# Three inner output projections of a four-layer trunk: the last block's second tile in two column halves, its pre-norm in one VectorE step

## The chip, the cores and the metric

One Trainium2 chip, one core. The metric is the device time of one execution of the program in microseconds (us). A profile of one execution accompanies the times; all rows below are of that execution. Engines are called PE (TensorE), DVE (VectorE), ACT (ScalarE), POOL (GpSimd) and SP (the queue that issues most loads).

## What is computed

A trunk of four layers on x (512 positions, 1024 channels, float32), each layer with another token mixer:

```python
for i in range(4):
    h = rmsnorm(x, pre_norm[i])
    y = branch_i(h, ...)          # mixer and gate, then  (...) @ w_out
    x = x + rmsnorm(y, post_norm[i])
```

```python
def rmsnorm(x, g):
    xf = x.astype(jnp.float32)
    y = xf * lax.rsqrt(jnp.mean(xf * xf, axis=-1, keepdims=True) + EPS)
    return (y * g.astype(jnp.float32)).astype(x.dtype)
```

The change is in the seam between two layers: the product with `w_out` (1024 x 1024), the post-norm and residual, and the pre-norm of the next layer. There are three such inner seams (behind layers 0, 1 and 2) and an outer one at the end, which has no next layer.

## The kernel before

**Arithmetic.** Every float32 matrix product is made of three TensorE products of rounded parts: a tensor `a` is split into `aH` (a rounded copy, by ACT) and `aL = a - aH` (by DVE or POOL), and `aH bH + aH bL + aL bH` is accumulated in a PSUM bank. Activations are kept transposed as `XH` and `XL`, by blocks of 128 positions.

**Weights.** They come as a stream of chunks in one fixed order. SP loads a chunk into one of two `wraw` buffers; a split puts it into a pair `wh`, `wl` (two pairs, and one more pair of buffers for chunks with the tag "x"). For some chunks the split is cut in four parts and the subtraction is spread: "mix" gives the four parts to POOL, DVE, POOL, DVE; "late" gives all four to POOL, and its casts go to ACT two at a time. In the seam, the chunks c0 and c1 hold the first 512 output columns, c2 and c3 the second 512 (each chunk holds half of the contraction); c2 has the tag "x". The next layer's first chunk ("mix") and second chunk ("late", tag "x") are split while block 3 is computed, by `split_later` (L168), which hands out the steps one by one.

**The projection, `out_proj` (L317).** Loop `t` runs over four blocks of 128 positions, and once more (t = 4) to finish the last. A block has two output tiles of 128 x 512 (n = 0 and 1), each of 24 matmuls: 12 with one chunk, 12 with the other. The engines run pipelined over blocks: in pass t, PE computes block t's tiles and transposes block t-2; u = t-1 is the block whose norm is being finished, v = t-2 the block that is transposed.

Names along the path of block 3, in their order:

- `y_stat(t, n)` (L357): ACT squares a PSUM tile and sums it into `ssq`; `y_gain` (L360): DVE multiplies the tile by the post-norm gain into `yg`.
- `y_root(t)` (L365): nine small DVE instructions of 128 x 1, each waiting for the one before, give the root `rs[t]`.
- `x_new(t, n)` (L368): DVE updates the residual, `xt = yg * rs + xt`.
- `x_stat(t, n)` (L373): ACT squares the new half of x; POOL multiplies it by the next layer's gain into `hblk`.
- `x_root(t)` (L380): nine small DVE instructions again; `x_scale(t, n)` (L383): ACT scales `hblk` by the root.
- `transposes` (L268): eight PE transposes of a block, in two banks; `x_high` (L277): ACT copies them into `XH`; `x_low` (L281): DVE writes `XL`.

In pass 4 PE has no tile of the projection left. It runs the first tiles of the next layer's first product on blocks 0 and 1 (`nxt`), one in each of three places, then the transposes of block 3, then a fourth such tile.

**Order.** Instructions through `act_`, `dve_`, `pool_`, `pe_` keep the order in which they are written, each on its engine; the rest is placed by a planner. All of `out_proj` except casts and subtractions of some chunks is written out this way. PSUM has eight banks; `bank()` takes a free one. `last_tile` (L331), for the outer projection alone, already computes its second tile of block 3 in two column halves.

Of the kernel before, what the change touches and what calls it, by code (L numbers as in the profile page):

```python
# [10 lines left out]
F32 = mybir.dt.float32  # L11
# [3 lines left out]
AF = mybir.ActivationFunctionType  # L15
ALU = mybir.AluOpType
MUL, ADD, SUB, MAX = ALU.mult, ALU.add, ALU.subtract, ALU.max
# [30 lines left out]
def tile_hybrid_trunk(ctx: ExitStack, tc: tile.TileContext, I, out, depth=4):  # L48
# [22 lines left out]
    act_, dve_, pool_, pe_ = (Engine(e, True) for e in engines)  # L71
# [14 lines left out]
    sm = ctx.enter_context(tc.tile_pool(name="sm", bufs=8))  # L86

    def bank():
        return ps.tile([128, 512], F32, name="bank", tag="bank")
# [78 lines left out]
    def split_later():  # L168

        i = state["split"]  # L170
        if i == len(stream):
            return iter(())
        if state["load"] == i:
            do_load(stream[i])
            state["load"] += 1
        state["split"] += 1
        stream[i]["steps"] = split_steps(stream[i])
        return stream[i]["steps"]
# [102 lines left out]
    def x_low(bvs, t, dve=dve):  # L281
        for kk, bv in enumerate(bvs):
            dve.tensor_tensor(out=XL[:, t, 4 * kk:4 * kk + 4, :], in0=bv,
                              in1=XH[:, t, 4 * kk:4 * kk + 4, :].bitcast(F32), op=SUB)
# [32 lines left out]
    def out_proj(pre, x, begin, tail, emit_x, nxt):  # L317


        ssq = [sm.tile([128, 2], F32, name="ssq") for t in range(4)]  # L320
        yg, hs, sss, rs, bvs = {}, {}, {}, {}, {}
        more = nxt is not None
        roots = bank()

        def cs(n):
            return slice(512 * n, 512 * n + 512)

        def mms(*a, **kw):
            out_mms(*pre.S, *a, **kw)
# [24 lines left out]
        def junk():  # L354
            return yp.tile([128, 512], BF16, name="junk", tag="junk", bufs=2)[:]
# [4 lines left out]
        def y_gain(t, n, bt):  # L360
            y = yg0[:, t, :] if n == 0 else yp.tile([128, 512], F32, name="yg1", bufs=2)[:]
            dve_.tensor_tensor(out=y, in0=bt[:], in1=gpost[:, cs(n)], op=MUL)
            yg[t, n] = y
# [9 lines left out]
        def x_stat(t, n):  # L373
            if n == 0:
                hs[t] = yp.tile([128, 1024], F32, name="hblk", tag="hblk", bufs=2)
                sss[t] = sm.tile([128, 2], F32, name="ssq")
            act_.activation(out=junk(), in_=x[:, t, cs(n)], func=AF.Square, scale=1.0 / 32, accum_out=sss[t][:, n:n + 1])
            pool_.tensor_tensor(out=hs[t][:, cs(n)], in0=x[:, t, cs(n)], in1=gpre[:, cs(n)], op=MUL)

        def x_root(t):  # L380
            rs[t] = rsqrt(sss[t][:, 0:1], 1, 1.0, 1, sss[t][:, 1:2], dve_, pb=roots[:, 8 * t + 4:8 * t + 7])

        def x_scale(t, n):  # L383
            act_.activation(out=hs[t][:, cs(n)], in_=hs[t][:, cs(n)], func=AF.Copy, scale=rs[t])

        while len(pre.bts) < 4:
# [5 lines left out]
        yp, gpost, gpre = begin()  # L392
        yg0 = yp.tile([128, 4, 512], F32, name="yg0")
        c1, c2 = get(), get()
        w = split_later()
        for t in range(5 if more else 4):

            u, v = t - 1, t - 2
            if t == 0:
                for _ in w:  # L400
                    pass
                c3 = get()
            if u >= 0:
                y_stat(u, 1, bt)
                y_root(u)
            if more and v >= 0:
                x_scale(v, 1)
            if t == 4:
                for _ in w:
                    pass  # L410
            if t < 4:
                mms(bts[t], t, 1, c1, True, range(2))
            else:
                next(nxt, None)
            if more and v >= 0:
                bvs[v] = transposes(hs[v], pe_)
            if t < 4:
                mms(bts[t], t, 1, c1, True, range(2, 4))
            else:
                next(nxt, None)  # L420
            if more and v >= 0:
                x_high(bvs[v], v, act_)
            if t < 4:
                y_stat(t, 0, bts[t])
            if u >= 0:
                x_new(u, 0)
                y_gain(u, 1, bt)
                if more:
                    x_stat(u, 0)
                x_new(u, 1)  # L430
                if more:
                    x_stat(u, 1)
            if t < 4:
                y_gain(t, 0, bts[t])
            if t == 3 and not more:
                last_tile()
                break
            if t < 4:
                bt = bank()
                mms(bt, t, 0, c2, False)  # L440
                if t == 3 and more:
                    w = split_later()
            if more and u >= 0:
                x_root(u)
            if more and v >= 0:
                x_low(bvs[v], v, dve_)
            for _ in w:
                pass
            if t < 4:
                mms(bt, t, 1, c3, True)  # L450
            else:
                next(nxt, None)
            if more and u >= 0:
                if t == 3:
                    w = split_later()
                    next(w, None)
                    next(w, None)
                x_scale(u, 0)
        if more:
            x_scale(3, 1)  # L460
# [1613 lines left out]
```

## Time and profile before

| | us |
|---|---|
| median of three runs | 989.39 |
| the two lower of these runs | 989.27, 989.39 |
| the profiled execution | 988.71 |
| its span, first to last instruction | 986.9 |
| PE busy (matmuls) | 949.0 |
| DVE, ACT, POOL busy | 619.3, 510.6, 444.7 |

The mean granted clock of TensorE is 0.985 of full speed. A row of a timeline gives the start of an instruction from the beginning of the span, its duration, engine, line, operation, what it writes and reads, its shape, how many follow each other as one row (x2), and in brackets the engine's idle time before it with what ended it. Where a helper records the operation, the line is that of the helper (L66); the tile names tell the instructions apart: `bank<-ssq` is the first instruction of a root, `xt<-yg,rs_y,xt` is x_new, `XL<-bank,XH` is x_low, `wl<-wraw,wh` a weight split, `hblk<-hblk,rs_y` is x_scale. A second instruction can be recorded as starting a little before the end of the one ahead of it.

### The profile page before, as it was taken

Reading aid. Unit: us, or ns where it says so; the run is one execution under the profiler, and the core shown is the slowest. Engines: PE = TensorE matmul, PEld = TensorE weight load, DVE = VectorE, ACT = ScalarE, POOL = GpSimd, SP = SyncE. Lnnn points to the kernel's source line nnn. Section 1 sums busy time; section 2 is a strip of 40 time slices with the busy share of each in tenths; the row PEclk is TensorE's granted clock in tenths of the full one; section 3 lists DMA queues with packets and bytes.
Section 4 is the critical chain, followed back from the end, with each engine's and each line's share of the span. In section 5 each row is a group of like instructions: output and inputs, shape, how many; then the busy total and the mean of one; then the engine's idle time right before and its main releaser. Section 6 shows DMA issues by size and latency. Waiting matters only on the chain.

```text
span 986.9 us, 14348 instructions
## 1 busy us (share of the span) xinstructions
PE 949.0 (96%) x5319; PEld 784.0 (79%) x5319; DVE 619.3 (63%) x1431; ACT 510.6 (52%) x1133; POOL 444.7 (45%) x337
## 2 busy tenths in 40 slices
PE   7959999999999999999999999999999999999997
PEld 6858988778889888887897877778767778888876
DVE  7899796855686866676820345666576857314365
ACT  4547777734367665663643243675683752222231
POOL 6677585656554131333646351714364535411120
PEclk8979999999999999999999999999999999999998
DMA  9211111435418232123124422110126033323021
GB/s 243 83 43 44 44 43 44 171 124 122 149 62 217 86 128 86 43 86 129 45 80 136 121 66 72 48 50 20 67 70 232 27 103 100 114 93 120 6 81 65
DMA packets 69366, 90.40 MB, mean 92 GB/s; under 512 B 13608, under 2 KB 49584, under 8 KB 69168
## 3 DMA queue, kind: packets, MB, share of 16 engines
q1 hardware_dynamic: 66944, 80.63, 26.6%
q10 hardware_dynamic: 2352, 8.85, 2.4%
q8 instruction: 42, 0.69, 0.3%
q14 instruction: 28, 0.23, 0.1%
HBM read 83.44 MB, written 4.98 MB: 90 GB/s over the span
## 4 chain that ended last, share of the span: by engine, by line
PE 74%; DVE 14%; ACT 5%; issue 3%; POOL 3%; DMA 0%; POOLq 0%; ACTq 0%; DVEq 0%; SPq 0%
PE bank L66 22%; PE bank L218 9%; PE bank L217 9%; PE bank L216 9%; PE bank L1841 4%; PE bank L1842 4%; PE bank L1843 4%; PE bank L101 4%; PE bank L1731 3%; DVE bank L66 2%; DVE xt L66 2%; PE bank L1773 2%; PE bank L1524 1%; DVE wl L66 1%; DVE rs_y L66 1%
## 5 line engine op out<-in xcount | busy, mean ns | idle before, releaser
L160 POOL TENSOR_TENSOR wl<-wraw,wh 128x2048 fp32r<-128x2048 f32 (+3 forms) x37 | 139.2, 3767 | 250.7 <-ACT wh L156 231.8
L216 PE MATMUL bank<-XH,wh 128*128 128x512 f32 (+1 forms) x526 | 183.2, 350 | 0.1
L218 PE MATMUL bank<-XH,wl 128*128 128x512 f32 (+1 forms) x526 | 181.5, 345 | 1.1 <-POOL wl L160 0.9
L217 PE MATMUL bank<-XL,wh 128*128 128x512 f32 (+1 forms) x526 | 181.0, 344 | 0.7 <-DVE XL L1660 0.7
L66 POOL TENSOR_TENSOR wl<-wraw,wh 128x512 fp32r<-128x512 f32 (+1 forms) x63 | 93.8, 1513 | 93.3 <-ACT wh L66 74.7
L66 PE MATMUL bank<-wh,XH 128*128 128x512 f32 (+1 forms) x328 | 114.0, 360 | 0.8 <-ACT g L66 0.8
L66 PE MATMUL bank<-wl,XH 128*128 128x512 f32 (+1 forms) x328 | 111.3, 352 | 0.3
L218 PEld LDWEIGHTS bank<-XH,wl 128*128 128x128 f32 x526 | 99.1, 188 | 15.2 <-POOL wl L160 1.5
L66 PE MATMUL bank<-wh,XL 128*128 128x512 f32 (+1 forms) x328 | 110.4, 349 | 0.6 <-POOL XL L227 0.6
L217 PEld LDWEIGHTS bank<-XL,wh 128*128 128x128 f32 x526 | 99.2, 189 | 13.3 <-DVE XL L1660 1.1
L216 PEld LDWEIGHTS bank<-XH,wh 128*128 128x128 f32 x526 | 99.1, 189 | 13.1 <-ACT XH L1659 0.6
L156 ACT CAST wh<-wraw 128x2048 fp32r<-128x2048 f32 (+3 forms) x50 | 71.0, 1439 | 51.0 <-PE bank L217 21.0
L66 DVE TENSOR_TENSOR wl<-wraw,wh 128x512 fp32r<-128x512 f32 x42 | 58.2, 1420 | 30.8 <-ACT wh L66 30.5
L1841 PE MATMUL bank<-wh,XH 128*128 128x512 f32 x192 | 76.5, 398 | 0.0
L1842 PE MATMUL bank<-wl,XH 128*128 128x512 f32 x192 | 76.0, 396 | 0.1
L1843 PE MATMUL bank<-wh,XL 128*128 128x512 f32 x192 | 75.8, 395 | 0.0
L66 PEld LDWEIGHTS bank<-wl,XH 128*128 128x128 f32 x328 | 61.5, 193 | 10.5 <-POOL wl L66 3.3
L66 PEld LDWEIGHTS bank<-wh,XH 128*128 128x128 f32 x328 | 61.6, 194 | 9.1 <-ACT g L66 1.1
L66 PEld LDWEIGHTS bank<-wh,XL 128*128 128x128 f32 x328 | 60.8, 191 | 9.2 <-POOL XL L227 1.1
L66 ACT CAST wh<-wraw 128x512 fp32r<-128x512 f32 (+1 forms) x105 | 59.3, 636 | 11.2 <-DMA wraw<-in_a_w_out_dram 7.7
L66 POOL TENSOR_TENSOR hblk<-xt,gpre 128x512 f32<-128x512 f32 x24 | 32.3, 1351 | 58.3 <-DVE xt L66 58.3
L160 DVE TENSOR_TENSOR wl<-wraw,wh 128x2048 fp32r<-128x2048 f32 (+2 forms) x13 | 20.7, 1618 | 42.8 <-ACT wh L156 42.7
(361 smaller groups left out, 2071.1 us busy)
## 6 DMA issues: line engine op xcount, KB each, us to landing
wraw<-in_d_w_in_dram SPq DMA_DIRECT2D x12, 1024.0 KB, 5.1
wraw<-in_b_w_in_dram SPq DMA_DIRECT2D x9, 1024.0 KB, 5.2
wraw<-in_c_w_in_dram SPq DMA_DIRECT2D x8, 1024.0 KB, 5.6
wraw<-in_a_w_in_dram SPq DMA_DIRECT2D x7, 1024.0 KB, 5.3
wraw<-in_c_w_uq_dram SPq DMA_DIRECT2D x8, 576.0 KB, 4.3
wraw<-in_a_w_glu_dram SPq DMA_DIRECT2D x4, 1024.0 KB, 5.0
wraw<-in_a_w_out_dram SPq DMA_DIRECT2D x4, 1024.0 KB, 5.1
wraw<-in_b_w_out_dram SPq DMA_DIRECT2D x4, 1024.0 KB, 4.9
```

The source lines that it names most:

```text
L66: return lambda *a, **k: after(f(*a, **k))
L101: pe.matmul(out_ap, lhsT=in_ap, rhs=ident[0:k, 0:k], is_transpose=True, start=True, stop=True)
L156: (act_ if c["eng"] in MIX else act).copy(h, r)
L160: es[(i + k) % len(es)].tensor_tensor(out=l, in0=r, in1=h.bitcast(F32), op=SUB)
L216: pe.matmul(out_ap, lhsT=lh, rhs=rh, start=(i == 0), stop=False)
L217: pe.matmul(out_ap, lhsT=lh, rhs=rl, start=False, stop=False)
L218: pe.matmul(out_ap, lhsT=ll, rhs=rh, start=False, stop=(i == n - 1))
L1731: pe.matmul(where[n], lhsT=qT[:, h % 2, 128 * n:128 * n + 128], rhs=kT[:, h, 0:128 * (n + 1)], start=True, stop=True)
L1773: after(pe.matmul(ob[64 * e:64 * e + 64, 128 * kb:512], lhsT=vs[:, kb, 64 * h:64 * h + 64], rhs=PT2[e][:, off[kb]:off[kb] + 4 - kb, :], st ...
L1841: pe.matmul(bt[:], lhsT=xh, rhs=H[:, k, :], start=(i == 0 and k == 0), stop=False)
L1842: pe.matmul(bt[:], lhsT=xh, rhs=L[:, k, :], start=False, stop=False)
L1843: pe.matmul(bt[:], lhsT=xl, rhs=H[:, k, :], start=False, stop=(i == 1 and k == 3))
```

## The change

In the three inner projections, for block 3:

- its second tile is computed as two halves of 256 columns, `half[0]` and `half[1]`, each in a bank of its own and each through c2 and then c3; so the order on PE is c2, c3, c2, c3 with 12 matmuls of 256 columns each;
- `y_stat_half` and `y_gain_half` do for a half what `y_stat` and `y_gain` do for a tile. Those of half 0 stand, on ACT, behind the six casts of the next layer's chunks and, on DVE, behind the two subtractions of the "mix" chunk; an addition joins half 0's sum to that of the first tile. Those of half 1 come in pass 4, and the root is made from the sums;
- the product with the next layer's gain on POOL and the scaling on ACT are replaced by one DVE instruction for each 512 columns, `hblk = (x * rs) * gpre`, behind the root;
- `x_low` of block 2 stands ahead of `x_root(3)`, no longer behind it;
- the "late" chunk's first split steps are handed out between the halves' matmuls, no longer behind the whole tile.

```diff
--- before.py
+++ after.py
@@ -375,12 +375,17 @@
                 hs[t] = yp.tile([128, 1024], F32, name="hblk", tag="hblk", bufs=2)
                 sss[t] = sm.tile([128, 2], F32, name="ssq")
             act_.activation(out=junk(), in_=x[:, t, cs(n)], func=AF.Square, scale=1.0 / 32, accum_out=sss[t][:, n:n + 1])
-            pool_.tensor_tensor(out=hs[t][:, cs(n)], in0=x[:, t, cs(n)], in1=gpre[:, cs(n)], op=MUL)
+            if t < 3:
+                pool_.tensor_tensor(out=hs[t][:, cs(n)], in0=x[:, t, cs(n)], in1=gpre[:, cs(n)], op=MUL)
 
         def x_root(t):
             rs[t] = rsqrt(sss[t][:, 0:1], 1, 1.0, 1, sss[t][:, 1:2], dve_, pb=roots[:, 8 * t + 4:8 * t + 7])
 
         def x_scale(t, n):
+            if t == 3:
+                dve_.scalar_tensor_tensor(out=hs[t][:, cs(n)], in0=x[:, t, cs(n)], scalar=rs[t], in1=gpre[:, cs(n)],
+                                          op0=MUL, op1=MUL)
+                return
             act_.activation(out=hs[t][:, cs(n)], in_=hs[t][:, cs(n)], func=AF.Copy, scale=rs[t])
 
         while len(pre.bts) < 4:
@@ -400,7 +405,10 @@
                 for _ in w:
                     pass
                 c3 = get()
-            if u >= 0:
+            if t == 4:
+                y_stat_half(1)
+                rs[3] = rsqrt(part[:, 1:2], 1, 1.0, 1, ssq[3][:, 1:2], dve_, pb=roots[:, 24:27])
+            elif u >= 0:
                 y_stat(u, 1, bt)
                 y_root(u)
             if more and v >= 0:
@@ -424,7 +432,10 @@
                 y_stat(t, 0, bts[t])
             if u >= 0:
                 x_new(u, 0)
-                y_gain(u, 1, bt)
+                if t == 4:
+                    y_gain_half(1)
+                else:
+                    y_gain(u, 1, bt)
                 if more:
                     x_stat(u, 0)
                 x_new(u, 1)
@@ -435,26 +446,48 @@
             if t == 3 and not more:
                 last_tile()
                 break
-            if t < 4:
+            if t == 3:
+
+                half = [bank(), bank()]
+                part = sm.tile([128, 2], F32, name="ssq")
+                yg[3, 1] = yp.tile([128, 512], F32, name="yg1", bufs=2)[:]
+
+                def y_stat_half(hf):
+                    act_.activation(out=junk()[:, 0:256], in_=half[hf][:, 0:256], func=AF.Square, scale=1.0 / 32,
+                                    accum_out=part[:, hf:hf + 1])
+
+                def y_gain_half(hf):
+                    dve_.tensor_tensor(out=yg[3, 1][:, 256 * hf:256 * hf + 256], in0=half[hf][:, 0:256],
+                                       in1=gpost[:, 512 + 256 * hf:768 + 256 * hf], op=MUL)
+
+                mms(half[0], 3, 0, c2, False, cols=slice(0, 256))
+                w = split_later()
+            elif t < 4:
                 bt = bank()
                 mms(bt, t, 0, c2, False)
-                if t == 3 and more:
-                    w = split_later()
+            if t == 4:
+                x_low(bvs[v], v, dve_)
             if more and u >= 0:
                 x_root(u)
-            if more and v >= 0:
+            if more and 0 <= v < 2:
                 x_low(bvs[v], v, dve_)
             for _ in w:
                 pass
-            if t < 4:
+            if t == 3:
+                w = split_later()
+                mms(half[0], 3, 1, c3, True, cols=slice(0, 256))
+                next(w, None)
+                next(w, None)
+                mms(half[1], 3, 0, c2, False, cols=slice(256, 512))
+                y_stat_half(0)
+                y_gain_half(0)
+                dve_.tensor_tensor(out=ssq[3][:, 1:2], in0=ssq[3][:, 0:1], in1=part[:, 0:1], op=ADD)
+                mms(half[1], 3, 1, c3, True, cols=slice(256, 512))
+            elif t < 4:
                 mms(bt, t, 1, c3, True)
             else:
                 next(nxt, None)
             if more and u >= 0:
-                if t == 3:
-                    w = split_later()
-                    next(w, None)
-                    next(w, None)
                 x_scale(u, 0)
         if more:
             x_scale(3, 1)
```

## Rows read from the trace of the kernel before

**Rows 1.** Head of the page: the span and the number of instructions.

```profile
span 986.9 us, 14348 instructions
```

**Rows 2.** Waits of PE, whole span: engine, line, releaser, us in total, times, longest.

```profile
PE bank L66 <- ACT hblk L66: 3.3, 4, 1.1
```

**Rows 3.** Timeline of PE, second inner projection: start, duration, instruction, idle before.

```profile
496.19 1.27 PE L66 MATMUL bank<-ident,hblk 128*128 128x128 f32 x8 [0.82 <-ACT hblk L66]
```

**Rows 4.** Timeline of ACT, second inner projection.

```profile
482.44 3.21 ACT L66 CAST wh<-wraw 128x512 fp32r<-128x512 f32 x6
...
486.18 0.58 ACT L66 ACTIVATE junk<-bank 128x512 bf16<-128x512 f32 x1
...
489.24 1.07 ACT L66 CAST XH<-bank 128x512 fp32r<-128x512 f32 x2 [0.75 <-PE bank L66]
...
495.42 1.34 ACT L66 ACTIVATE hblk<-hblk,rs_y 128x512 f32<-128x512 f32 x2 [1.98 <-DVE rs_y L66]
```

**Rows 5.** Timeline of DVE, second inner projection.

```profile
486.20 1.78 DVE L66 TENSOR_TENSOR wl<-wraw,wh 128x512 fp32r<-128x512 f32 x1
487.90 0.21 DVE L66 TENSOR_SCALAR bank<-ssq 128x1 f32<-128x1 f32 x1
...
489.58 0.16 DVE L66 SCALAR_TENSOR_TENSOR rs_y<-bank,rs_y 128x1 f32<-128x1 f32 x1
489.78 1.14 DVE L66 SCALAR_TENSOR_TENSOR xt<-yg,rs_y,xt 128x512 f32<-128x512 f32 x1
...
491.55 1.07 DVE L66 SCALAR_TENSOR_TENSOR xt<-yg,rs_y,xt 128x512 f32<-128x512 f32 x1
493.47 0.22 DVE L66 TENSOR_SCALAR bank<-ssq 128x1 f32<-128x1 f32 x1 [0.85 <-ACT junk L66]
...
495.24 1.28 DVE L66 TENSOR_TENSOR XL<-bank,XH 128x512 fp32r<-128x512 f32 x2
```

**Rows 6.** Timeline of DVE, last projection, where POOL does nothing.

```profile
966.83 0.75 DVE L66 SCALAR_TENSOR_TENSOR xt<-yg,rs_y,xt 128x512 f32<-128x512 f32 x1
...
977.39 0.42 DVE L66 TENSOR_TENSOR yg<-bank,gpost 128x256 f32<-128x256 f32 x1 [0.81 <-ACT junk L66]
977.74 0.15 DVE L66 TENSOR_TENSOR ssq<-ssq 128x1 f32<-128x1 f32 x1
```

**Rows 7.** Timeline of POOL, second inner projection.

```profile
490.32 1.75 POOL L66 TENSOR_TENSOR wl<-wraw,wh 128x512 fp32r<-128x512 f32 x1
492.03 1.74 POOL L66 TENSOR_TENSOR hblk<-xt,gpre 128x512 f32<-128x512 f32 x1
```

**Rows 8.** Timeline of DVE and of POOL in the first layer, around 34.4 us.

```profile
34.37 1.32 DVE L66 TENSOR_TENSOR mq<-mq,kq 128x32 f32<-128x32 f32 x1
...
34.36 1.28 POOL L66 TENSOR_TENSOR wl<-wraw,wh 128x512 fp32r<-128x512 f32 x1
```

**Rows 9.** Timeline of PE: a whole tile, then two halves; first and last matmul.

```profile
479.74 0.39 PE L66 MATMUL bank<-wh,XH 128*128 128x512 f32 x1
...
485.10 0.39 PE L66 MATMUL bank<-wh,XL 128*128 128x512 f32 x1
...
973.78 0.28 PE L66 MATMUL bank<-wh,XH 128*128 128x256 f32 x1
...
979.37 0.28 PE L66 MATMUL bank<-wh,XL 128*128 128x256 f32 x1
```

**Rows 10.** Timeline of DVE and of POOL, first inner projection.

```profile
294.92 1.13 DVE L66 SCALAR_TENSOR_TENSOR xt<-yg,rs_y,xt 128x512 f32<-128x512 f32 x1
...
298.91 0.22 DVE L66 TENSOR_SCALAR bank<-ssq 128x1 f32<-128x1 f32 x1 [1.16 <-ACT junk L66]
...
295.47 1.73 POOL L66 TENSOR_TENSOR wl<-wraw,wh 128x512 fp32r<-128x512 f32 x1
```

**Rows 11.** Busy time by stretch: us, five engines' busy us, PEclk, DMA share, GB/s.

```profile
50.00:60.00 10.00, 4.65 (x32) 3.81 (x33) 10.00 (x27) 5.59 (x13) 8.90 (x12) 0.67 0.35 105
...
476.00:496.00 20.00, 19.35 (x126) 17.12 (x124) 17.14 (x50) 13.52 (x31) 14.44 (x10) 1.00 0.30 90
```

## The prediction

> **What bounds the kernel now.** I read the head of the page first: the span is 986.9 us [rows 1], and the profiled execution took 988.71, so 1.81 us lie around the span. The median of the runs shown is 989.39, that is 0.68 above the profiled execution; I make the sum against 988.71 and add 0.68 at the end. Next I read what PE waits for. Waits on `hblk` come to 3.3 us in four pieces [rows 2], so whatever the change does to the last block's tail, it cannot give back more than 3.3 us unless PE itself gets shorter work. The timeline of the second inner projection shows one such piece: PE idles 0.82 us before the transposes of block 3 at 496.19, and it is ACT's scaling of `hblk` that ends the wait [rows 3].
>
> What is behind that wait is a chain on DVE and ACT. Going back from it: ACT scales the two halves in 1.34 us from 495.42 [rows 4]; DVE's x_root(3) starts at 493.47 after 0.85 us of waiting for ACT's Square [rows 5]; x_new(3,1) ends at 491.55 + 1.07 = 492.62; x_new(3,0) runs from 489.78; y_root(3) starts at 487.90, straight behind DVE's second weight split of 1.78 us, which ends at 487.98. So the chain starts on a busy DVE, not on PE.
>
> The reader is to see one thing more here. The same x_new takes 0.75 us in the last projection [rows 6], but 1.14 and 1.07 here. In this stretch POOL runs its weight splits. Its last one ends at 490.32 + 1.75 = 492.07, and x_new(3,1) ends 0.55 later; the next POOL instruction, started at 492.03, takes 1.74 us, and a POOL instruction of that size alone takes 1.28 [rows 7, 8]. The two engines take turns, whole instructions at a time. x_new(3,1) therefore ends when POOL lets it, and not when DVE gets to it. The Trainium skill, "SBUF — State Buffer", section "Who interferes with whom", says it as a rule: a VectorE instruction with two SBUF inputs and a GpSimd instruction that reads SBUF take the shared port pair as an exclusive lock, and whichever starts first blocks the other to its end. The rows agree with it: 0.55 us behind the other's end each time.
>
> **The change part by part**, for the second projection; block 3 is the last.
>
> *The two column halves on PE.* 24 matmuls of 512 columns start from 479.74 to 485.10, so 5.36/23 = 0.233 us each; 48 of 256 columns start from 973.78 to 979.37, so 5.59/47 = 0.119 each [rows 9]. The tile costs 48 x 0.119 - 24 x 0.233 = +0.12 us. It lies before PE's wait of 0.82 [rows 3], which hides it; without that cover, 0.4 us for three projections.
>
> *ACT.* One Square of 512 columns (0.58 us) becomes two of 256; at worst both cost as much, so +0.6 us ahead of x_scale(2,1) and two weight casts. ACT then has 0.75 us of idle time before its next XH copy [rows 4], which hides it. Two scalings leave ACT (1.34 us) and two products leave POOL: the products ran during x_root(3), and no wait stands behind them.
>
> *What comes ahead of y_root(3) on DVE.* y_gain_half(0) and the addition of the partial sums now stand behind the weight split. In the last projection the half product starts at 977.39, the addition 0.35 later and takes 0.15 [rows 6]; a dependent instruction follows 0.04 behind another's end (489.58 + 0.16, then 489.78) [rows 5]. So y_root(3) starts 0.35 + 0.15 + 0.04 = 0.53 to 0.54 us later, and x_new(3,0) asks at 490.31 to 490.32 in place of 489.78.
>
> *Whether that delay reaches the end.* POOL's last split has its recorded start at 490.32 [rows 7]. If DVE asks first, everything is as before: x_new(3,0) runs when POOL's last-but-one split is done, POOL's last split behind it to 492.07. y_gain_half(1) (0.42) then lets x_new(3,1) ask at about 491.3, before 492.07, and it ends at 492.62 again. The 0.53 cost nothing, and the 0.26 that the half product saves brings nothing. In the first projection the same sum is 294.92 + 0.53 = 295.45 against POOL's 295.47 [rows 10]. The margin is 0.00 to 0.02 us. The price if it is lost is a rival below. I take DVE first, since the finer of the two margins is not negative and the other is in its favour. If the engines merely slowed each other, x_new(3,1), asked 0.53 - 0.26 = 0.27 later and taking 0.75 to 1.07, would end between 0.05 earlier and 0.27 later than now.
>
> *x_low(2) moved ahead of x_root(3).* Its two instructions take 1.28 us [rows 5], and one that doesn't depend on the one before starts 0.08 before its end (487.98, then 487.90). x_root(3) starts at 492.62 - 0.08 + 1.28 - 0.08 = 493.74 instead of 493.47: +0.27, since the wait for the Square that it fills is only 0.85 long. In the first projection that wait is 1.16 (a DMA issue stands in ACT's queue there) and x_root(3) started at 298.91 [rows 10]; 298.91 - 1.16 + 1.12 = 298.87, so nothing. The third repeats the second.
>
> *x_scale(3) on DVE.* From x_root's first instruction to the next dependent step are 489.78 - 487.90 = 1.88 us. The form is x_new's: 0.75, the second starting 0.67 after the first. The second half is ready 1.88 + 0.67 + 0.75 = 3.30 us after x_root's start; with ACT it was 495.42 + 1.34 - 493.47 = 3.29. So +0.01. POOL is quiet by then; one POOL instruction in the way would cost at most its own 1.3.
>
> *Where the stall goes.* PE's wait grows from 0.82 to some 1.0. x_high(3) and x_low(3) follow the transposes as before, covered by the same matmuls, and later work depends on PE, so the shift reaches the end.
>
> *Slots.* PE reads c2 to the end of the third quarter of the tile, 479.74 + 36 x 0.119 = 484.0, instead of its middle; the tagged weight buffer that c2 lies in is wanted by ACT's fifth cast, at 482.44 + 4 x 0.53 = 484.6 [rows 4]. Queued behind that cast are x_scale(2) and POOL's last four splits. With 0.6 of room it costs nothing. The extra PSUM bank makes seven in use (roots, two of transposes, block 3's first tile, block 2's second, two halves) of eight.
>
> **Sum.** Second and third projection 0.27 + 0.01 = +0.28 each, first +0.01: +0.57 us. 988.71 + 0.57 = 989.28, as a median 989.39 + 0.57 = about 990.0.
>
> **The rivals.**
> 1. *Slower: POOL takes its turn first.* Place: x_new(3,0) against POOL's last weight split. It decides when DVE asks after 490.32, so 0.01 us is enough. Early in the trace a DVE instruction of 32 columns that started at 34.37, 0.01 behind a POOL split of 1.28, took 1.32 [rows 8]: the later one waits out the other. Then POOL's split ends at 490.32 + 1.28 = 491.60, x_new(3,0) at 492.15, y_gain_half(1) at 492.50, x_new(3,1) asks at 492.54 and, POOL now empty, ends at 493.29: 0.67 later than now. Three times 0.67 on top of 0.57 is +2.6: 992.0. By the rule cited, too, who starts first decides: 990.0 or 992.0.
> 2. *Faster: the wait goes.* The chain could lose all of PE's wait: at most 3.3 us [rows 2], 986.1 as a median. For it: half of the reduction leaves the tail, and two engines' steps become one. Against it: the Square and product of half 0 were never what y_root(3) waited for (DVE's split was), and POOL's product ended (492.03 + 1.74 + 1.28 = 495.05) before the root at 495.4.
> 3. *The change's early half doesn't come early, or is paid for:* a slot for the second half or c2's buffer frees late, or the order planned for the instructions around it moves. A wait of a cast's 0.53 to 1 us per projection gives 991.5 to 993.
> 4. *Slower by more: TensorE's clock.* From 50 to 60 us, with PE busy 4.65 of 10, the granted clock averaged 0.67, between the two levels of 1.2 and 2.4 GHz; from 476 to 496, with the 0.82 wait in it, it was 1.00 [rows 11]. If waits of 1.0 to 1.7 us made it fall, and each fall cost what that stretch lost (0.33 of 10 us), it were three times 3.3: about 1000. Nothing says that waits this short do it.
>
> **How the numbers follow.** Forecast (DVE first) 0.50, its own range 989.2 to 991.2 (with the 0.05 less to 0.27 more above for each projection, and 0.3 between executions). Rival 1 0.27, rival 2 0.12, rival 3 0.08, rival 4 0.03. The predicted time is 990.0. The range takes in rival 1 with the same spread and part of rival 2: 988.2 to 992.6, which leaves out the stronger gains, the clock and the longer waits of rival 3. About 2% (20 us) is what a measurement of this kernel can tell from no change; all but unforeseen outcomes stay within it: faster 0.01, same 0.97, slower 0.02.
>
> **What would show it.** Right: x_new(3,0) ends 0.55 after POOL's last-but-one split and x_new(3,1) 0.55 after its last; x_root(3) starts at once behind x_low(2) in the second and third projection; PE's wait, now for DVE, is 0.2 to 0.3 longer there and unchanged in the first. Wrong: POOL's last split takes 1.28 instead of 1.75 while x_new(3,0) takes about 1.8 (rival 1); no PE wait before block 3's transposes (rival 2); a wait on PE inside the two halves, or on ACT before its fifth cast (rival 3); a granted clock under 1.00 behind the waits (rival 4).

## The result, and the profile after

Over ten executions the changed kernel takes 994.42 us as a median (991.58 to 996.52); the kernel before, on the same chips, 989.32. The ratio is 1.0053, 95% interval [1.0044, 1.0062]: about 5 us slower, which is within 2%, and above the predicted range of 988.2 to 992.6. The profiled execution took 996.25, so it is one of the longer ones; 1.75 lie around its span.

The head of the page (to be set beside [rows 1]) and what PE waits for (beside [rows 2]):

```profile
span 994.5 us, 14493 instructions
...
PE bank L66 <- DVE hblk L66: 5.6, 3, 2.0
...
PE bank L66 <- ACT hblk L66: 0.4, 1, 0.4
```

The span is 7.6 us longer. The 3.3 us of [rows 2] were 0.4 outside the inner seams and 1.15, 0.82 and 0.95 in them, 2.92 together. The 0.4 is still there; the three seams now cost 5.6, so 2.6 us more. PE's timeline shows them, the second being the one of [rows 3]:

```profile
302.71 1.14 PE L66 MATMUL bank<-ident,hblk 128*128 128x128 f32 x5 [1.79 <-DVE hblk L66]
...
499.57 1.10 PE L66 MATMUL bank<-ident,hblk 128*128 128x128 f32 x6 [1.79 <-DVE hblk L66]
...
800.26 1.01 PE L66 MATMUL bank<-ident,hblk 128*128 128x128 f32 x6 [1.97 <-DVE hblk L66]
```

What lies behind the wait of 1.79 in the second projection is DVE's timeline, the part that answers to [rows 5]. The reader is to see the addition, `ssq<-ssq`, at 490.71:

```profile
488.67 1.78 DVE L66 TENSOR_TENSOR wl<-wraw,wh 128x512 fp32r<-128x512 f32 x1
490.38 0.41 DVE L66 TENSOR_TENSOR yg<-bank,gpost 128x256 f32<-128x256 f32 x1
490.71 0.91 DVE L66 TENSOR_TENSOR ssq<-ssq 128x1 f32<-128x1 f32 x1
491.73 0.22 DVE L66 TENSOR_SCALAR bank<-ssq 128x1 f32<-128x1 f32 x1
...
493.62 1.03 DVE L66 SCALAR_TENSOR_TENSOR xt<-yg,rs_y,xt 128x512 f32<-128x512 f32 x1
494.57 0.41 DVE L66 TENSOR_TENSOR yg<-bank,gpost 128x256 f32<-128x256 f32 x1
495.02 0.75 DVE L66 SCALAR_TENSOR_TENSOR xt<-yg,rs_y,xt 128x512 f32<-128x512 f32 x1
495.69 1.28 DVE L66 TENSOR_TENSOR XL<-bank,XH 128x512 fp32r<-128x512 f32 x2
496.89 0.21 DVE L66 TENSOR_SCALAR bank<-ssq 128x1 f32<-128x1 f32 x1
...
498.77 1.41 DVE L66 SCALAR_TENSOR_TENSOR hblk<-xt,rs_y,gpre 128x512 f32<-128x512 f32 x2
```

Beside it stand POOL's last three weight splits of this seam, in the timeline of POOL (the last is the one of 490.32 in [rows 7]):

```profile
489.87 1.73 POOL L66 TENSOR_TENSOR wl<-wraw,wh 128x512 fp32r<-128x512 f32 x1
...
491.56 1.29 POOL L66 TENSOR_TENSOR wl<-wraw,wh 128x512 fp32r<-128x512 f32 x1
...
492.81 1.29 POOL L66 TENSOR_TENSOR wl<-wraw,wh 128x512 fp32r<-128x512 f32 x1
```

The addition starts at 490.71, in the middle of POOL's split that ends at 489.87 + 1.73 = 491.60, and ends at 490.71 + 0.91 = 491.62. So an instruction that reads two numbers in each partition, 0.15 us long in [rows 6], waits for POOL's turn to end, as a large one does. The root then starts at 491.73, 0.11 behind it. From the end of DVE's split (488.67 + 1.78 = 490.45) to the request of x_new(3,0) it takes 493.62 - 490.45 = 3.17 us; in [rows 5] it was 489.78 - 487.98 = 1.80. The 1.37 us of delay bring the request to 0.81 behind the start of POOL's last split at 492.81. That split takes 1.29, undisturbed, ends at 494.10, and x_new(3,0) ends 0.55 behind it. Then POOL has nothing left, and x_new(3,1) takes 0.75.

The rest of the extra time is TensorE's clock. The windows behind the three waits, kernel before first (us, busy time of PE, PEld, DVE, ACT and POOL with their instructions, PEclk, DMA share, GB/s):

```profile
302.00:312.00 10.00, 10.00 (x86) 9.80 (x85) 4.38 (x4) 7.64 (x13) 3.00 (x2) 1.00 0.94 226
500.00:510.00 10.00, 10.00 (x87) 10.00 (x86) 1.79 (x2) 5.08 (x10) 2.49 (x2) 1.00 0.11 40
801.00:811.00 10.00, 10.00 (x45) 8.05 (x44) 3.80 (x7) 2.54 (x3) 1.10 (x1) 1.00 0.34 105
```

and after:

```profile
302.00:312.00 10.00, 9.29 (x66) 9.12 (x67) 4.61 (x6) 5.85 (x10) 2.38 (x2) 0.83 0.71 167
500.00:510.00 10.00, 9.99 (x73) 9.77 (x71) 1.53 (x3) 2.25 (x4) 0.00 (x0) 0.83 0.22 80
801.00:811.00 10.00, 10.00 (x48) 8.14 (x48) 6.50 (x11) 5.64 (x9) 4.35 (x3) 0.83 0.00 1
```

The clock was granted in full there before, and is 0.83 in each of the three windows after: about 3.4 of 10 us at the 1.2 GHz level instead of 2.4. (In the 30 us from 290, 490 and 790 it was 1.00 before and is 0.94 after, so no fall of before is missed by where the windows lie.) A window at 0.83 loses 0.17 x 10 = 1.7 us of clock, and that bounds the price of a fall. What a fall cost can be read from PE: block 0's transposes start at 272.41, 468.09 and 766.21 before and at 272.86, 470.58 and 771.21 after, so the two stretches from one seam to the next, and the one to the end of the span, are 2.04, 2.51 and 2.5 us longer. Less the longer waits (0.64, 0.97 and 1.02), that leaves 1.4 to 1.5 us for each fall. So the 7.6 us of span are 2.6 of waits, some 4.5 of clock, and 0.4 by which this execution is late before the first seam. In other executions fewer of these falls must happen, since their times go from 991.6 to 996.5 and the median is 5.1 above before. Only one execution has a trace, but the mean clock of each is on record: 0.980 to 0.982 in the three above 996 us, 0.984 to 0.987 in the other seven.

### The profile page after: what moved, and what is told of

The parts are those of the page before. It is cut to its first block, busy times and chain, and to the rows that moved or that the text cites. A ratio compares the mean times of both kernels' runs of the same rounds, so it can differ in the third digit from the quotient of the medians.

```text
span 994.5 us, 14493 instructions
## 1 busy us (share of the span) xinstructions
PE 953.6 (96%) x5391; PEld 791.8 (80%) x5391; DVE 625.1 (63%) x1443; ACT 507.2 (51%) x1133; POOL 434.5 (44%) x331
## 4 chain that ended last, share of the span: by engine, by line
PE 74%; DVE 15%; ACT 4%; issue 3%; POOL 3%; DMA 0%; ACTq 0%; DVEq 0%; SPq 0%; POOLq 0%
PE bank L66 23%; PE bank L218 9%; PE bank L217 9%; PE bank L216 9%; PE bank L1874 4%; PE bank L1875 4%; PE bank L1876 4%; PE bank L101 4%; PE bank L1764 3%; DVE bank L66 2%; DVE xt L66 2%; PE bank L1806 2%; PE bank L1557 1%; DVE wl L66 1%; DVE rs_y L66 1%
## 5 line engine op out<-in xcount | busy, mean ns | idle before, releaser
L66 PE MATMUL bank<-wh,XH 128*128 128x256 f32 (+1 forms) x344 | 116.7, 351 | 0.8 <-ACT g L66 0.8
L66 PE MATMUL bank<-wl,XH 128*128 128x256 f32 (+1 forms) x344 | 113.9, 343 | 0.3
L66 PE MATMUL bank<-wh,XL 128*128 128x256 f32 (+1 forms) x344 | 113.1, 340 | 0.6 <-POOL XL L227 0.6
L66 PEld LDWEIGHTS bank<-wl,XH 128*128 128x128 f32 x344 | 64.4, 193 | 9.9 <-POOL wl L66 3.3
L66 PEld LDWEIGHTS bank<-wh,XH 128*128 128x128 f32 x344 | 64.6, 194 | 8.6 <-ACT g L66 1.1
L66 PEld LDWEIGHTS bank<-wh,XL 128*128 128x128 f32 x344 | 63.7, 190 | 8.5 <-POOL XL L227 1.1
L66 POOL TENSOR_TENSOR hblk<-xt,gpre 128x512 f32<-128x512 f32 x18 | 23.3, 1294 | 58.1 <-DVE xt L66 58.1
```

The lines of the kernel that those rows point to most:

```text
L66: return lambda *a, **k: after(f(*a, **k))
```

## The experiments

Theory A: the 128 x 1 addition takes turns with POOL, because both its operands lie in SBUF; its delay makes x_new(3,0) lose its turn, and behind the longer waits the clock falls. Theory B, the first rival: the half product alone is late enough for x_new(3,0) to lose its turn, and the addition is cheap. Theory C: the DVE step (`hblk` in one instruction, x_low(2) ahead of the root) is what costs. The three waits named below are those of PE in the three inner seams, in order; before they are 1.15, 0.82 and 0.95.

### The addition: taken away, alone, and with one operand in PSUM

**Taken away (e1).** The changed kernel, with the addition left out; the root's first instruction adds the two sums itself, as per-partition scalars. (Not shown: the form of the root that takes two sums, and epsilon, which is added to the first tile's sum earlier.)

```diff
-                rs[3] = rsqrt(part[:, 1:2], 1, 1.0, 1, ssq[3][:, 1:2], dve_, pb=roots[:, 24:27])
+                rs[3] = rsqrt(part[:, 1:2], 1, 1.0, 1, (ssq[3][:, 0:1], part[:, 0:1]), dve_, pb=roots[:, 24:27])
...
-                dve_.tensor_tensor(out=ssq[3][:, 1:2], in0=ssq[3][:, 0:1], in1=part[:, 0:1], op=ADD)
```

> The changed kernel without its 128x1 addition on DVE: the three sums meet in the root's first instruction, which takes two per-partition scalars, and epsilon is added to the first sum earlier. Theory 1 (the addition reads two SBUF operands and waits its turn behind a POOL weight split, 0.90 us instead of 0.15; that delay loses the next turn too, and PE's longer waits let its clock fall): x_new(3,0) asks 0.34 us later than in the kernel before, ahead of POOL's last split, so it ends where it ended before; PE waits for block 3's hblk 1.1 to 1.2 us in each of the three projections (3.5 in all against 5.6 with the addition), the granted clock stays at 1.00 behind them, and the time is 0.6 us over the kernel before, ratio 1.000 to 1.001. Theory 2 (the loss is the extra DVE and ACT work of the halves and of x_scale as such): the waits stay at 1.8 to 2.0 us each and the ratio at about 1.005.

Measured: 990.21, ratio 1.0007 [0.9998, 1.0015]. Waits 1.11, 1.12 and 1.28. DVE, then POOL, second projection:

```profile
487.09 0.27 DVE L66 TENSOR_SCALAR bank<-ssq 128x1 f32<-128x1 f32 x1
...
489.02 0.76 DVE L66 SCALAR_TENSOR_TENSOR xt<-yg,rs_y,xt 128x512 f32<-128x512 f32 x1
...
490.15 1.33 DVE L66 SCALAR_TENSOR_TENSOR xt<-yg,rs_y,xt 128x512 f32<-128x512 f32 x1
...
486.25 1.74 POOL L66 TENSOR_TENSOR wl<-wraw,wh 128x512 fp32r<-128x512 f32 x1
...
487.95 1.28 POOL L66 TENSOR_TENSOR wl<-wraw,wh 128x512 fp32r<-128x512 f32 x1
...
489.19 1.74 POOL L66 TENSOR_TENSOR wl<-wraw,wh 128x512 fp32r<-128x512 f32 x1
```

x_new(3,0) asks at 489.02, POOL's last split at 489.19: DVE is first, POOL's split takes 1.74 and x_new(3,1) ends 0.55 behind it (490.15 + 1.33 = 491.48 against 490.93). This is the order that the prediction forecast, with the time that it forecast, and the waits have changed by -0.04, +0.30 and +0.33 where it had +0.01, +0.28 and +0.28. It speaks against B and C: all else of the change is in this kernel, and it costs 0.7 us (by the interval's upper end 1.5). Behind the 1.12 the granted clock stays at 1.00. One thing more is in these rows: the root's first instruction reads three 128 x 1 operands in SBUF, two of them as per-partition scalars, starts at 487.09 in the middle of the POOL split of 486.25, and takes 0.27. So the per-partition scalars did not make it take turns; "two SBUF operands" here means operands other than these.

**Alone (e2).** The kernel before, with one unused addition of that form ahead of y_root(3).

```diff
                     next(w, None)
+                    part = sm.tile([128, 2], F32, name="ssq")
+                    dve_.tensor_tensor(out=part[:, 0:1], in0=ssq[3][:, 0:1], in1=ssq[2][:, 0:1], op=ADD)
                 x_scale(u, 0)
```

> The kernel before with nothing but one addition of two 128x1 SBUF operands put on DVE behind the second weight subtraction of pass 3, in each inner projection; its result is not used. Theory 1: this one instruction takes 0.9 to 1.25 us, since it starts inside a POOL weight split; x_new(3,0) then asks behind the start of POOL's last split, x_new(3,1) ends 0.7 to 1.4 us later than now, and PE's three waits grow from 0.8-1.15 to 1.5-2.5 us each: 2 to 4 us, and up to 1.7 us more for each wait behind which the clock falls. Ratio 1.002 to 1.009. Theory 2: an addition costs 0.2 us of DVE time, hidden by x_new's wait for POOL; ratio 1.000.

Measured: 996.76, ratio 1.0077 [1.0065, 1.0089]; waits 2.65, 2.35 and 2.44, and in the windows 302:312, 500:510 and 801:811 a granted clock of 0.83, 0.83 and 0.86. The addition, and the POOL split beside it:

```profile
489.93 1.24 DVE L66 TENSOR_TENSOR ssq<-ssq 128x1 f32<-128x1 f32 x1
...
492.96 1.22 DVE L66 SCALAR_TENSOR_TENSOR xt<-yg,rs_y,xt 128x512 f32<-128x512 f32 x1
...
494.83 1.29 DVE L66 SCALAR_TENSOR_TENSOR xt<-yg,rs_y,xt 128x512 f32<-128x512 f32 x1
...
489.42 1.73 POOL L66 TENSOR_TENSOR wl<-wraw,wh 128x512 fp32r<-128x512 f32 x1
```

The addition asks at 489.93 and ends at 491.17, 0.02 behind POOL's split (489.42 + 1.73 = 491.15). One instruction of 128 x 1 makes the kernel 7.6 us slower (0.0077 x 989.5). It is more than the whole change: the three waits are together 1.9 us longer than there. POOL still has the product of `hblk` here, which x_new(3,1) at 494.83 has to let pass as well; it takes 1.29 for 0.75, so most of the 1.9 is this.

**With one operand in PSUM (e7).** The changed kernel; ACT's sum over half 0 goes into a column of the PSUM bank `roots`.

```diff
-                                    accum_out=part[:, hf:hf + 1])
+                                    accum_out=roots[:, 64:65] if hf == 0 else part[:, 1:2])
...
-                dve_.tensor_tensor(out=ssq[3][:, 1:2], in0=ssq[3][:, 0:1], in1=part[:, 0:1], op=ADD)
+                dve_.tensor_tensor(out=ssq[3][:, 1:2], in0=ssq[3][:, 0:1], in1=roots[:, 64:65], op=ADD)
```

> The changed kernel with one thing different: ACT puts half 0's sum into PSUM, so that the addition, still in its place, reads one operand from SBUF and one from PSUM. Theory 1: the addition takes 0.15 to 0.2 us instead of 0.90, so it was the operand's place and not the instruction that cost. x_new(3,0) then asks 0.53 to 0.6 us later than in the kernel before, within 0.05 us of the start of POOL's last split: if it comes first, waits of 1.1 to 1.3 us each and ratio 1.000 to 1.001; if POOL does, x_new(3,0) ends about 1.2 us later, waits of 1.5 to 2.0 us and ratio 1.002 to 1.005. Rival (any instruction at that place is held up): 0.9 us again, ratio 1.005.

Measured: 994.15, ratio 1.0056 [1.0041, 1.0071]: as slow as the changed kernel. DVE, then POOL's split beside the addition and its last one:

```profile
488.92 0.14 DVE L66 TENSOR_TENSOR ssq<-ssq,bank 128x1 f32<-128x1 f32 x1
489.17 0.22 DVE L66 TENSOR_SCALAR bank<-ssq 128x1 f32<-128x1 f32 x1
...
491.06 1.78 DVE L66 SCALAR_TENSOR_TENSOR xt<-yg,rs_y,xt 128x512 f32<-128x512 f32 x1
...
488.07 1.74 POOL L66 TENSOR_TENSOR wl<-wraw,wh 128x512 fp32r<-128x512 f32 x1
...
491.01 1.28 POOL L66 TENSOR_TENSOR wl<-wraw,wh 128x512 fp32r<-128x512 f32 x1
```

The first half of theory A holds: with one operand in PSUM the addition takes 0.14 in the middle of a POOL split (488.07 to 489.81). Its second half was too simple. x_new(3,0) asks at 491.06, POOL's split at 491.01, so DVE loses its turn by 0.05 us, x_new(3,0) takes 1.78, and the waits are 1.83, 1.73 and 1.95. The 0.05 are lost between the addition's end (489.06) and the root's first instruction (489.17): 0.11 us, where the prediction had put 0.04. The order decides, not the size of the delay: 0.8 us late or 0.05 us late costs the same 2.6 us of waits.

### The parts alone

**The halves alone (e3).** The changed kernel with POOL's product, ACT's scaling and the old place of x_low(2) put back.

```diff
-            if t < 3:
+            if True:
                 pool_.tensor_tensor(out=hs[t][:, cs(n)], in0=x[:, t, cs(n)], in1=gpre[:, cs(n)], op=MUL)
...
         def x_scale(t, n):
-            if t == 3:
-                ...
...
-            if t == 4:
-                x_low(bvs[v], v, dve_)
...
```

> The column halves alone, with the addition; the product with the next gain stays on POOL, the scaling on ACT, x_low(2) behind x_root(3). Theory 1: the addition takes 0.9 us, x_new(3,0) loses its turn; POOL's product of the first half then takes a turn ahead of x_new(3,1), which the changed kernel does not have, so the waits are at least as long as there: 1.8 to 2.3 us each, clock falls behind some of them, ratio 1.004 to 1.009. Theory 2 (the DVE step in place of POOL and ACT is what costs): waits of about 1 us, ratio 1.000 to 1.001.

Measured: 998.16, ratio 1.0085 [1.007, 1.01]; addition 0.90, waits 2.62, 2.30 and 2.72, two of them longer than expected. x_new(3,1) and POOL's product:

```profile
494.09 1.55 DVE L66 SCALAR_TENSOR_TENSOR xt<-yg,rs_y,xt 128x512 f32<-128x512 f32 x1
...
493.80 1.29 POOL L66 TENSOR_TENSOR hblk<-xt,gpre 128x512 f32<-128x512 f32 x1 [0.63 <-DVE xt L66]
```

After the lost turn x_new(3,1) meets POOL's product, started at 493.80, and takes 1.55 instead of 0.75. So the DVE step, which takes that product away from POOL, does not cost in the changed kernel: x_new(3,1) is 0.8 us shorter with it, and the three waits together 2.1 us (7.6 here against 5.6). That speaks against theory C.

**The step alone (e4), and without the moved x_low(2) (e8).** The kernel before with `hblk = (x * rs) * gpre` on DVE for block 3 (as in the diff of the change); in e4 x_low(2) is moved ahead of x_root(3), in e8 it stands behind x_scale(3, 1):

```diff
...
+            x_low(bvs[2], 2, dve_)
             bvs = transposes(hs[3], pe_)
```

> The other part alone: the scaling by root and next gain in one DVE instruction per half, and x_low(2) ahead of x_root(3); the second tile stays whole, with no addition. Theory 1: x_new(3,0) and x_new(3,1) end where they end in the kernel before; x_root(3) starts 0.27 us later in the second and third projection and not in the first; PE waits 1.15, 1.1 and 1.2 us; the clock stays at 1.00; ratio 1.000 to 1.001. Theory 2: the waits are 1.5 us or more in all three projections, ratio over 1.002.

> The DVE step alone (no halves, no addition), with x_low(2) behind x_scale(3,1) instead of ahead of x_root(3). By the sum of the prediction x_root(3) starts 0.27 us earlier in the second and third projection than with x_low(2) ahead, PE's waits are 1.2, 0.9 and 1.0 us, and the time equals the kernel before: ratio 0.999 to 1.001. Rival (x_low(2) fits into the wait for the Square at no cost): the waits are 1.2, 1.2 and 1.3 as with x_low(2) ahead.

Measured: e4 989.06, ratio 1.0003 [0.9994, 1.0011], waits 1.21, 1.19 and 1.28; e8 989.49, ratio 1.0004 [0.9995, 1.0012], waits 1.25, 0.89 and 1.02. The root of x behind x_new(3,1), e4:

```profile
491.94 1.06 DVE L66 SCALAR_TENSOR_TENSOR xt<-yg,rs_y,xt 128x512 f32<-128x512 f32 x1
492.92 1.27 DVE L66 TENSOR_TENSOR XL<-bank,XH 128x512 fp32r<-128x512 f32 x2
494.12 0.21 DVE L66 TENSOR_SCALAR bank<-ssq 128x1 f32<-128x1 f32 x1
```

and e8:

```profile
492.14 1.07 DVE L66 SCALAR_TENSOR_TENSOR xt<-yg,rs_y,xt 128x512 f32<-128x512 f32 x1
494.06 0.22 DVE L66 TENSOR_SCALAR bank<-ssq 128x1 f32<-128x1 f32 x1 [0.85 <-ACT junk L66]
```

In e4 the root starts 494.12 - 493.00 = 1.12 behind x_new(3,1), in e8 0.85: the 0.27 us that the prediction worked out for x_low(2) ahead. In PE's waits it is 0.30 and 0.26 in the second and third seam and nothing in the first. The times can't tell the two apart.

### The clock

**Work for PE in the wait (e5).** The changed kernel, with 14 unused matmuls of 256 columns ahead of block 3's transposes.

```diff
+            fill = bank()
+            for _ in range(14):
+                pe_.matmul(fill[:, 0:256], lhsT=XH[:, 0, 0, :], rhs=XH[:, 0:2, 0, :], start=True, stop=True)
             bvs = transposes(hs[3], pe_)
```

> The changed kernel with 14 more matmuls of 256 columns on PE, ahead of block 3's transposes in each inner projection (14 x 0.119 = 1.67 us of work in waits of 1.8 to 2.0 us; their result is not used). The chain on DVE is not touched, so the transposes start as late as in the changed kernel. Theory clock (part of the loss is that PE's granted clock falls to the lower level behind the longer waits, 3.4 us at half speed, up to 1.7 us each): the granted clock stays at 1.00 behind the projections and the time falls to what the waits alone give, 2.6 us over the kernel before: ratio 1.002 to 1.003, with less spread between executions than the changed kernel's 991.6 to 996.5. Rival (the rest of the loss has another cause): ratio about 1.005 as in the changed kernel, or more by the added work.

Measured: 991.93 (990.38 to 993.14), ratio 1.0031 [1.0019, 1.0043]. The windows around the three seams (columns as above):

```profile
290.00:320.00 30.00, 29.61 (x233) 28.22 (x232) 21.02 (x38) 20.82 (x35) 12.87 (x8) 1.00 0.73 194
490.00:520.00 30.00, 29.80 (x220) 27.99 (x219) 11.00 (x25) 12.41 (x23) 13.35 (x9) 1.00 0.33 99
790.00:820.00 30.00, 29.79 (x147) 24.26 (x146) 16.97 (x33) 12.67 (x18) 9.00 (x5) 1.00 0.39 127
```

Nothing of the chain has changed (the addition is 0.90 long here too), only that PE is busy while it waits; the clock stays at 1.00, and the ratio falls from 1.0053 to 1.0031. So of the 5.1 us of the median about 0.0022 x 989 = 2.2 are the clock's, and some 3 are the waits'. The two ratios have intervals of 0.0009 and 0.0012 to either side, so the 2.2 is known to about 1.5 us. The traces give 2.6 for the waits, which leaves 2.5 for the clock: between one and two falls of 1.4 to 1.5 us in the median execution.

Over all runs, the waits of up to 1.29 us at this place (before, e1, e4, e6, e8, e9, e10) were followed by a granted clock of 1.00 in the stretches that were read. Behind the waits of 1.7 us and more it mostly fell, but not always: three times of three in the changed kernel and in e2, two of three in e3 and in e7, where the first seam kept 1.00 behind 2.62 and 1.83 us. What beside the wait decides is open.

### Better than both

**x_new with one operand in PSUM (e6).** The kernel before; block 3's two gain products are written back into their PSUM banks, so that x_new reads only `xt` from SBUF.

```diff
-            y = yg0[:, t, :] if n == 0 else yp.tile([128, 512], F32, name="yg1", bufs=2)[:]
+            if t == 3 and more:
+                y = bt[:]
+            else:
+                y = yg0[:, t, :] if n == 0 else yp.tile([128, 512], F32, name="yg1", bufs=2)[:]
```

> The kernel before, but block 3's two products with the post-norm gain are written back into their own PSUM banks, so that x_new(3,0) and x_new(3,1) read one operand from PSUM and only one from SBUF. Theory 1 (an instruction with two SBUF operands takes turns with POOL, one with a single SBUF operand does not): both x_new take 0.7 to 0.75 us beside POOL's splits instead of 1.13 and 1.07, x_new(3,1) ends 0.8 us earlier, PE's waits of 1.15, 0.82 and 0.95 us shrink to under 0.4 each; ratio 0.997 to 0.999. Rival (DVE and POOL slow each other whatever the operands' place): the durations stay over 1 us, ratio 1.000.

Measured: 987.32, ratio 0.9985 [0.9976, 0.9993]; waits 0.46, 0.12 and 0.27, the first a little above the expected 0.4. DVE, then POOL:

```profile
490.08 0.75 DVE L66 SCALAR_TENSOR_TENSOR xt<-bank,rs_y,xt 128x512 f32<-128x512 f32 x1
490.75 0.69 DVE L66 TENSOR_TENSOR bank<-bank,gpost 128x512 f32<-128x512 f32 x1
491.47 0.75 DVE L66 SCALAR_TENSOR_TENSOR xt<-bank,rs_y,xt 128x512 f32<-128x512 f32 x1
...
489.38 1.28 POOL L66 TENSOR_TENSOR wl<-wraw,wh 128x512 fp32r<-128x512 f32 x1
...
490.63 1.29 POOL L66 TENSOR_TENSOR wl<-wraw,wh 128x512 fp32r<-128x512 f32 x1
```

The two engines run side by side, each at the duration that it has alone: 0.75 where [rows 5] had 1.14 and 1.07, 1.29 where [rows 7] had 1.75. It is the same edit in kind as e7's, at the instruction where the turn is lost. The root `rs`, a per-partition scalar in SBUF, did not count here either.

**One more weight split for POOL (e10), and both (e9).** In the seam's first split the fourth part goes from DVE to POOL, so that only one part stands ahead of the root on DVE; e10 is that alone, e9 that and e6.

```diff
+    MIX = {"mix": [pool_, dve_, pool_, dve_], "seam": [pool_, dve_, pool_, pool_], "late": [pool_] * 4, "vec": [dve_] * 4}
...
-    add("b_w_in", 1024, 256, eng="mix")
+    add("b_w_in", 1024, 256, eng="seam")
...
```

> The kernel before with block 3's two products written back into PSUM, and besides the fourth part of the seam's first weight split given to POOL instead of DVE. Theory 1: DVE has one split of two SBUF operands less to wait for, y_root(3) starts about 1 us earlier, x_new is free of POOL; POOL's row of splits ends within 0.5 us of where it did. PE's waits for hblk before block 3's transposes come to less than 0.4 us in all three projections together, and the time is 2.0 to 3.0 us under the kernel before: ratio 0.997 to 0.998. Rival (POOL is now last: its product of the second half ends after the root): waits of 0.5 us or more each, ratio 0.9985 or above.

> The kernel before with the fourth part of the seam's first weight split on POOL instead of DVE, x_new reading its product from SBUF as before. Theory 1: y_root(3) starts about 1 us earlier, but x_new(3,0) and x_new(3,1) still take turns with POOL and hold its splits up, so x_new(3,1) ends 0.3 to 0.5 us earlier and POOL's products of block 3 end 0.9 us later; waits 0.6 to 1.1 us each, ratio 0.999 to 1.001. Rival (it was DVE's queue alone): the gain is the full 1 us per projection, waits under 0.2, ratio 0.997.

Measured: e10 988.73, ratio 0.9999 [0.999, 1.0008], with waits of 0.95, 0.71 and 0.84, and 0.22 more between the two groups of transposes in the second and third seam; e9 985.75, ratio 0.9967 [0.9955, 0.9978], with waits of 0.22, 0.19 and 0.39. In e10 x_new still takes turns:

```profile
488.53 1.70 DVE L66 SCALAR_TENSOR_TENSOR xt<-yg,rs_y,xt 128x512 f32<-128x512 f32 x1
...
490.87 1.07 DVE L66 SCALAR_TENSOR_TENSOR xt<-yg,rs_y,xt 128x512 f32<-128x512 f32 x1
```

In e9 both take 0.75. DVE's part of the chain got shorter in e10, and it brought nothing that the time shows: x_new(3,0) asks 0.13 us behind the start of a POOL split (488.40) and takes 1.70. e9 is the best version of all. But its waits sum to 0.8 us, hardly less than e6's 0.85, and more than the expected 0.4; the rest of its lead on e6 (0.9967 against 0.9985, each against the kernel before on its own chip, intervals that still touch, so 1.8 us known to about 1.4) lies outside these three waits. Part of it is seen in PE's timeline ahead of them: block 2's transposes follow block 1's by 10.89 us in e9 (474.91, then 485.80) and by 10.86 in e10, but by 11.14 in the kernel before and 11.15 in e6; over the three seams it is 0.24 to 0.30 us each, some 0.8 in all. In the kernel before, the matmul that reads the weights' `wl` starts at 488.04, 0.06 behind the end of DVE's split of the fourth part and 0.30 behind the matmul ahead of it; in e9 and e10 no such gap stands there.

## Why the prediction was wrong

**The step that failed** is "What comes ahead of y_root(3) on DVE": y_gain_half(0), 0.35, the addition, 0.15, and the gap, 0.04. The first term was right (490.38 to 490.71 is 0.33). The addition measured 0.91. Its duration was taken from [rows 6], the last projection, whose heading says that POOL does nothing there; here it starts inside a POOL split. The prediction had the rule in hand, and used it for x_new: two SBUF operands, so it takes turns with POOL. It did not apply it to an instruction of 128 x 1 with two SBUF operands, and gave no reason for leaving it out. The rule that was cited (the Trainium skill, "SBUF — State Buffer", section "Who interferes with whom") names no size, and e2 and e7 agree with it at this one: 1.24 us with both operands in SBUF, 0.14 with one.

**The gap** was mis-sized as well: 0.11 us behind the addition, in the changed kernel and in e7, where 0.04 was taken from inside a root. With a margin of 0.00 to 0.02 that alone loses the turn, as e7 shows by its 0.05; so the prediction would have missed even with an addition of 0.15. The root's first instruction also needs ACT's sum over half 1, which the instructions inside a root do not. But in e7 that sum was done at 487.64, 1.5 us earlier, and in e1 (487.09) and in the kernel before (487.90) the root's first instruction, which needs a sum of ACT's there too, starts 0.08 before the end of the instruction ahead of it. So ACT's sum alone does not cost the 0.07, and what does is open. A margin of that size was no ground for giving "DVE first" 0.50.

**Rival 1 came true, at its price.** It gave 0.67 for x_new(3,1): from DVE's split to the end of x_new(3,1) it is 495.77 - 490.45 = 5.32 now and was 4.64, so 0.68. With 0.28 for the rest it expected a wait longer by 0.95 in the second seam; 1.79 - 0.82 is 0.97. The three waits grew by 2.6, the figure it gave. That is no luck, since a lost turn costs the same however late DVE asks; but the way there was another: it had DVE late by some 0.01 us, and DVE was late by 0.81, by the addition. Its point of decision, POOL's recorded start, held to 0.05 us in e7.

**Rival 4 came true on top**, behind waits of 1.79 to 1.97, just above the 1.0 to 1.7 that it named; the waits of up to 1.29 in e1 and e4 kept the clock. The chance of 0.03 was too low; the sentence that gave it no evidence was right, since no row of the kernel before has a wait of 1.8 us at such a place, but that speaks for an open question, not for an unlikely one. Its price was too high: 1.4 to 1.5 us for a fall, not 3.3. The two rivals were also not apart. The clock hangs on the longer wait, so rival 1 should have been priced with it: 2.6, and up to 4.5 more. With the clock left out, the range ended at 992.6, which takes in rival 1 alone but not the 994.42 measured.

**A sum that does not come out:** the terms named for the forecast's own range (0.05 less to 0.27 more for each projection, 0.3 between executions) give 989.55 to 991.1 around 990.0, not 989.2 to 991.2. The miss does not hang on it.

**Right:** the sum of +0.57 for the case that DVE goes first, shown by e1 (990.21, forecast 990.0); x_low(2) ahead, +0.27 in the second and third seam and nothing in the first (e4, e8); the step for `hblk`, forecast +0.01, measured 0.07 to 0.10 in e8's waits; the halves on PE, which cost nothing that shows (block 2's transposes follow block 1's by 11.12 us after, 479.96 to 491.08, and by 11.14 before); the slots, no wait on PE inside the halves; and that ACT's and POOL's saved work brings nothing by itself (e4, 1.0003), but POOL's does once a turn is lost (e3). The bound of 3.3 us for rival 2 stands, though only 2.9 of it lie in the inner seams: e6 takes back 2.1 of the 2.9 us of waits, by another way.

**Open:** how many of the three falls each execution has; why the first seam kept its clock in e3 and e7; the 0.07 us of the gap; about 1 us of e9's lead on e6, which is within the noise of the two ratios; and the 0.4 us by which the profiled execution of the changed kernel is already late after its first 90 us, far ahead of any seam.

## What to carry to other kernels

On DVE beside POOL, ask of each instruction where its operands lie before asking how large it is: two operands in SBUF (per-partition scalars aside) make it take turns, and a tiny instruction then costs what is left of the other's. Take a duration only from a stretch in which the other engine does the same as in the stretch that you cost. Where two engines take turns, an order that hangs on hundredths of a microsecond is a coin, and the better edit is one that ends the turns (one operand in PSUM, e6) over one that changes who comes first; and price a longer wait of PE with a fall of its clock behind it.

## What was not expected of the hardware

- A DVE addition of 128 x 1 took 0.15 us alone, 0.90 to 1.24 beside a POOL weight split, and 0.14 beside one with an operand in PSUM.
- x_new, 128 x 512 with two SBUF operands, took 0.76 to 1.78 beside POOL, by how much of POOL's instruction was left when it asked (0.21 us in e1, for the 0.76); with one of them in PSUM 0.75, and POOL's split 1.29 instead of 1.75.
- A 128 x 1 instruction of DVE whose further operands were per-partition scalars in SBUF did not wait: 0.27 us in the middle of a POOL split (e1).
- Behind waits of PE of 1.8 to 2.0 us, in a kernel that keeps PE busy on both sides, the granted clock fell to its lower level for about 3.4 us; each fall lost 1.4 to 1.5 us.
